# Four buffers for weight sums and split weights, splits three groups ahead, and another product order in the first MLP pair

## The chip, the core and the metric

The kernel runs on one core of a Trainium2 chip. A core has a matrix engine (TensorE, PE in the profile, with its weight loads shown apart as PEld), three engines for element work (VectorE or DVE, ScalarE or ACT, GpSimd or POOL), and SyncE (SP), which here issues nearly all DMA transfers. Each engine works through its own instructions in order and waits for the others on semaphores. Matmuls write to PSUM, everything else lives in SBUF. The metric is the device time of one execution in microseconds.

## The reference

One decoder layer over a sequence of 1024 positions with width 1024, in float32. Cut to what matters:

```python
h = rmsnorm(x, mix_norm)
proj = h @ w_in                                   # q, k, v, su, sv, g_a, g_b
y_att = sliding_window_attention(q, k, v, ...)     # 8 heads, window 128
y_sgu = chunked_spatial_gating(su, sv, ...)        # causal chunks of 128
merged = sigmoid(g_a) * (y_att @ w_oa) + sigmoid(g_b) * (y_sgu @ w_ob)
x = x + merged @ w_out
x = x + conv_gated_mlp(rmsnorm(x, ffn_norm), w_up, conv_w, conv_b, w_down)   # D_FF 2816
```

## The kernel before

**Arithmetic.** A float32 operand is split into a high part (a copy to the matmul's float type, on ACT, `copy_hi`, line 87) and a low part (operand less high part, on POOL or DVE), and a product is three matmuls: high by high, high by low, low by high. Besides, the large products are done in Strassen's manner as Winograd wrote it: a 2 by 2 block product with seven block products, named by the left operand (A11, A12, S1, S2, S3, S4, A22) with the right one (B11, B21, T1, T2, T3, B22, T4). In the gate and MLP stages a product (`prod`, line 1018) is 12 matmuls of 128 by 128 by 512. S1 to S4 are sums of weight blocks and must be made on the chip.

**Stages.** First come norm, projections, attention and spatial gating. Then eight gate pairs (one 128-row block of g_b and of g_a each; `gate_pair`, line 1112, makes the last seven, about 250 to 423 us), 16 jobs for the two branches (y @ w_ob and y @ w_oa, each times its gate, to 507 us), 14 groups for the output projection (`out_group`, line 1437, to 613 us), and 22 pairs of the MLP's up projection with its down projection between them. The first two MLP pairs are special: the first (`first_pair`, line 1570) finds its right operands only as the projection ends.

**Gate pairs and weight sums.** A gate pair computes A11, S3, A12, S1, A22, S2 and S4 in this order into halves of two PSUM tiles (zg with g0, g1 and zv with v0, v1). Its sums (`Blocks.sums`, 1029) and the scaling by the row norm run on DVE, its tanh on ACT (`gate_out`), from where the gate goes to DRAM. The next pair copies A11's result (x1, line 1124) to SBUF before A12 is added to the same PSUM half. In the same stage DVE prepares sums of weights that come later: 30 units, listed in `UNITS` (1044), a "u" unit for an MLP pair (two operations on 512 columns) and an "o" unit for the output projection (four on 256). A step (`sums_step`, 1066) first has SP load the next unit into one of two `ls` buffers (`sums_load`, 1051), then makes its own sums in place and stores them to DRAM (1077 for "u", 1084 for "o"). From the second of these pairs on there are three steps in a pair; the last ten units are made in the branches. In the sixth pair `ya_load` also fetches the attention's result (four loads).

**Jobs.** `run_jobs` (705) runs branches and output groups as one list. For job i it issues the matmuls, then the load of job i + 4, then, in an output group, the first part of the group's tail, then the split of job i + 2, and then the rest. An output group's tail is what its product releases (`ends` in `main`): `copies` after group 1 (M1 copied from one set of PSUM halves, X, to the other, Yb), `end_c11` after 3, `end_c22` after 9, `end_c12` after 11 and `end_c21` after 13. These add the residual, store x2, and build the MLP's right operands from it: high and low parts of B11, B21, B22 and T1 to T4. The last job of the list is `first_left`, which loads the first MLP pair's left operands; their splits (p for A11 and A12, s3, q for S1 and A22, and AX for S2 and S4) stand inside `end_c12`, `end_c21` and group 10's tail. A split weight (`woh`, `wol`) has two buffers.

**The first pair** makes A11, S3, S1, A12, S4, S2, A22. A11 and S2 share a PSUM half of zv with S3 and A22 beside it; copies to SBUF (x1, x7, u5, u2) free them.

The order of instructions within each engine is that of the program text; a tile framework puts the semaphores in.

## Time and profile before

| | us |
|---|---|
| median of 3 runs | 1277.44 (1274.58 to 1277.73) |
| the profiled execution | 1278.34 |
| its span | 1276.6 |
| PE busy in it | 1199.7 |
| DVE, POOL, ACT busy | 922.0, 588.3, 568.7 |
| mean granted PE clock | 0.974 |

The span runs from the first to the last instruction; 1.7 us lie around it. Where a row of a table by stage is cited, its start and end are us from the span's start. A row of the timeline gives start, length, engine, line, operation, out and in tiles with their shape, how many instructions it joins, and in brackets the idle time just before it with what ended it. SPq is SP's sequencer, where DMA issues stand in order.

### The profile page before, as it was taken

To read this page: it belongs to the slowest core of one execution; us is meant where nothing else is said; L and a number is where in the kernel's file an instruction comes from. 1 tells how busy PE (TensorE), PEld (TensorE's weight loads), DVE (VectorE), ACT (ScalarE), POOL (GpSimd) and SP (SyncE) were. 2 spreads that over 40 slices of the span, in tenths; PEclk is the share of its full clock that TensorE was granted. 3 is DMA by queue.
4 is the path that set the end of the run, shared out by engine and by line. 5 is a ranking of instruction groups with operands and counts; after the bars stand their busy time and mean duration, and the time that the engine had idled before them with its cause. 6 is when DMAs were issued, how large, how long until landed. Compare 5 with 4: busy or idle time off the path is not lost.

```text
span 1276.6 us, 16055 instructions
## 1 busy us (share of the span) xinstructions
PE 1199.7 (94%) x5842; PEld 1005.7 (79%) x5842; DVE 922.0 (72%) x1094; ACT 568.7 (45%) x883; POOL 588.3 (46%) x375
## 2 busy tenths in 40 slices
PE   8999999998897899995689999999999999999998
PEld 8989899876775688774467888888888888788887
DVE  7789948666547677474438887887887889686574
ACT  8555667623324112554344444444444445443432
POOL 2476673875556223353546566566566553000000
PEclk9999999999899899997789999999999999999999
DMA  7110150276786798642213233243233355986372
GB/s 269 31 38 32 53 217 16 69 244 226 236 294 208 267 338 300 205 168 74 74 42 116 99 125 126 106 132 122 99 119 129 109 178 185 368 300 206 117 227 94
DMA packets 92767, 202.82 MB, mean 159 GB/s; under 512 B 9744, under 2 KB 18192, under 8 KB 92688
## 3 DMA queue, kind: packets, MB, share of 16 engines
q1 hardware_dynamic: 92688, 201.80, 45.8%
q8 instruction: 46, 0.75, 0.2%
q14 instruction: 33, 0.27, 0.1%
HBM read 146.97 MB, written 54.79 MB: 158 GB/s over the span
## 4 chain that ended last, share of the span: by engine, by line
PE 63%; DVE 13%; DMA 6%; issue 6%; ACT 5%; POOL 4%; SPq 0%; ACTq 0%; POOLq 0%; DVEq 0%
PE pz L1022 32%; PE pd L1794 9%; PE pdy L1794 7%; DVE ls L620 3%; PE px L1450 3%; DMA ls<-wout 3%; DMA sum<-ls 2%; PE po L93 2%; PE po L91 2%; PE po L92 2%; POOL wol L1434 1%; DVE xa L620 1%; DVE pz L1038 1%; PE pu L93 1%; PE pu L91 1%
## 5 line engine op out<-in xcount | busy, mean ns | idle before, releaser
L1022 PE MATMUL pz<-T,qh 128*128 128x512 f32 x472 | 148.3, 396 | 5.4 <-DVE pz L1599 4.4
L620 DVE TENSOR_TENSOR ls<-ls 128x512 f32<-128x512 f32 (+1 forms) x76 | 81.4, 1071 | 58.5 <-DMA ls<-wup 29.8
L1022 PE MATMUL pz<-B,ph 128*128 128x512 f32 x352 | 110.0, 394 | 2.1 <-DVE tmp L1587 1.4
L982 POOL TENSOR_TENSOR pl<-lp,ph 128x1024 fp32r<-128x1024 f32 x30 | 72.2, 2407 | 86.1 <-ACT ph L87 85.9
L1022 PEld LDWEIGHTS pz<-T,qh 128*128 128x128 f32 x472 | 89.9, 191 | 25.4 <-DVE pz L1599 4.8
L1022 PE MATMUL pz<-T,ql 128*128 128x512 f32 x236 | 92.9, 394 | 0.0
L982 POOL TENSOR_TENSOR ql<-lq,qh 128x1024 fp32r<-128x1024 f32 x30 | 77.4, 2582 | 13.7 <-ACT qh L87 13.7
L1022 PE MATMUL pz<-T,s3h 128*128 128x512 f32 x232 | 73.4, 398 | 9.7 <-ACT tmp L1579 9.7
L1022 PEld LDWEIGHTS pz<-B,ph 128*128 128x128 f32 x352 | 65.4, 189 | 18.5 <-ACT x L1638 3.6
L1038 DVE TENSOR_TENSOR pz<-pz,rstd_b 128x1024 f32<-128x1024 f32 x60 | 74.0, 1232 | 7.4 <-ACT rstd_b L141 5.4
L982 POOL TENSOR_TENSOR s3l<-s,s3h 128x512 fp32r<-128x512 f32 x29 | 38.5, 1326 | 73.6 <-ACT s3h L87 73.6
L1022 PE MATMUL pz<-B,pl 128*128 128x512 f32 x176 | 68.6, 390 | 0.0
L1794 PE MATMUL pd<-bl,ah 128*128 128x512 f32 x176 | 68.5, 389 | 0.0
L1794 PE MATMUL pd<-bh,al 128*128 128x512 f32 x176 | 68.5, 389 | 0.0
L1794 PE MATMUL pd<-bh,ah 128*128 128x512 f32 x176 | 68.5, 389 | 0.0
L1022 PE MATMUL pz<-x,ph 128*128 128x512 f32 x128 | 45.6, 441 | 20.1 <-ACT x L1124 20.1
L1022 PE MATMUL pz<-B,AX 128*128 128x512 f32 x264 | 63.6, 390 | 0.8 <-DVE pz L1589 0.8
L1022 PE MATMUL pz<-T,AX 128*128 128x512 f32 x264 | 63.4, 389 | 0.0
L1434 POOL TENSOR_TENSOR wol<-wo,woh 128x1024 fp32r<-128x1024 f32 x14 | 34.5, 2465 | 55.9 <-ACT woh L87 55.9
L1022 PEld LDWEIGHTS pz<-T,s3h 128*128 128x128 f32 x232 | 44.5, 193 | 19.4 <-ACT tmp L1579 10.1
L1022 PEld LDWEIGHTS pz<-B,AX 128*128 128x128 f32 x264 | 49.5, 188 | 11.4 <-DVE pz L1589 1.2
L1022 PEld LDWEIGHTS pz<-T,AX 128*128 128x128 f32 x264 | 49.6, 188 | 10.3
(351 smaller groups left out, 3603.3 us busy)
## 6 DMA issues: line engine op xcount, KB each, us to landing
ls<-wup SPq DMA_DIRECT2D x22, 512.0 KB, 5.4
sum<-ls SPq DMA_DIRECT2D x22, 512.0 KB, 6.1
lp<-wup SPq DMA_DIRECT2D x22, 512.0 KB, 3.5
ra<-wdown SPq DMA_DIRECT2D x44, 256.0 KB, 5.0
b<-T SPq DMA_DIRECT2D x44, 256.0 KB, 4.0
B<-tv SPq DMA_DIRECT2D x33, 256.0 KB, 2.0
T<-tt SPq DMA_DIRECT2D x33, 256.0 KB, 2.0
b<-B SPq DMA_DIRECT2D x33, 256.0 KB, 3.3
```

Source lines behind the costliest of these rows:

```text
L91: nc.tensor.matmul(out, wh, mh, start=first, stop=False, **kw)
L92: nc.tensor.matmul(out, wh, ml, start=False, stop=False, **kw)
L93: nc.tensor.matmul(out, wl, mh, start=False, stop=last, **kw)
L620: eng.tensor_tensor(out, x, y, op=op)
L982: nc.gpsimd.tensor_tensor(l, r, h.bitcast(F), op=ALU.subtract)
L1022: nc.tensor.matmul(o, p[:, k, :], y[:, q, k, :], start=not more and k == 0 and j == 0, stop=k == 3 and j == 2, skip_group_check=True)
L1038: nc.vector.tensor_tensor(z, z, rstd_b, op=ALU.mult)
L1434: nc.gpsimd.tensor_tensor(l, r, h.bitcast(F), op=ALU.subtract)
L1450: nc.tensor.matmul(o[d], w[p][:, k, 128 * d:128 * d + 128], y[:, q, 2 * kp + k, :], start=s in ("M1", "M7") and kp == 0 and k == 0 and j == 0,
L1794: nc.tensor.matmul(o[d], p[:, k - k0, m], q[:, k - k0, :], start=new and k == 0 and j == 0, stop=k == HK - 1 and j == 2, skip_group_check= ...
```

## The change

The diff has three parts.

First, the weight sums. Units before the fourteenth rotate through four places, two `ls` buffers and two halves of a new tile `lsy` in the pool `big`; from unit 14 on the two `ls` buffers remain. `v_end` issues a second load, and step 12 issues none, so loads run two units ahead until then and one from there on. `ya_load` moves from the sixth pair to the seventh (c = 5 to c = 6), since the pool `big` has seven tiles.

On SP's queue, in the fourth of these gate pairs, before (`sum` is a unit's store to DRAM, `so` one of an "o" unit, `lq` the next pair's left operand, `dth` a gate's store):

```order
L1058 DMA ls_3558<-wup 128x512
L1059 DMA ls_3558<-wup 128x1024
L1077 DMA sum_3563<-ls_3511 128x1024
L97 DMA lq_3596<-wga 128x1024
L1097 DMA dth_3603<-th_3601 128x1024
L1062 DMA ls_3605<-wout 128x4x256
L1077 DMA sum_3609<-ls_3558 128x1024
L1058 DMA ls_3663<-wup 128x512
L1059 DMA ls_3663<-wup 128x1024
L1084 DMA so_2419<-ls_3605 512x1x256
```

The same stretch on SP's queue after the change:

```order
L1073 DMA ls_3558<-wout 128x4x256
L1089 DMA sum_3562<-lsy_3055 128x1024
L97 DMA lq_3595<-wga 128x1024
L1109 DMA dth_3602<-th_3600 128x1024
L1069 DMA lsy_3055<-wup 128x512
L1070 DMA lsy_3055<-wup 128x1024
L1089 DMA sum_3608<-ls_3511 128x1024
L1069 DMA lsy_3055<-wup 128x512
L1070 DMA lsy_3055<-wup 128x1024
L1096 DMA so_2419<-ls_3558 512x1x256
```

Each load now stands a step earlier: the "o" load that stood behind `lq` and `dth` stands ahead of both.

Second, the output projection. A group's preparation of others is put into a function `ahead`, which runs right after its matmuls and ahead of its whole tail: the right operand's split for group g + 2 (`m_prep`), the weight split for group g + 3, the load for group g + 6, the residual's load, and the first MLP pair's loads (group 10) and splits (groups 11 to 13). Split weights have four buffers: two `wst` ones, two halves of a tile `we`, and for groups 12 and 13 a tile `wl`. The squares' tile `sqt` moves to the pool `big`. The high and low parts of T2 move to the end of `end_c21`.

On ACT at groups 0 to 3, before (`woh` is a weight's high part, the copies of line 1330 are M1's, `rT` is m_prep's):

```order
L87 ACTIVATE woh_5000<-wo_4811 128x1024
L1330 COPY px_4966<-px_4964 128x512 x2
L1330 COPY px_4967<-px_4965 128x512
L87 ACTIVATE woh_5034<-wo_4851 128x1024
L1330 COPY px_4967<-px_4965 128x512
L87 ACTIVATE rT_645_5071<-m_4247 128x1024
L87 ACTIVATE woh_5074<-wo_4997 128x1024
```

And after:

```order
L87 ACTIVATE we<-wo_4806 128x1024
L87 ACTIVATE we<-wo_4846 128x1024
L87 ACTIVATE woh_5030<-wo_4997 128x1024
L1341 COPY px_4962<-px_4960 128x512 x2
L1341 COPY px_4963<-px_4961 128x512 x2
L87 ACTIVATE rT_638_5065<-m_4242 128x1024
L87 ACTIVATE woh_5068<-wo_5000 128x1024
```

Three weight splits (groups 2, 3 and 4) now stand ahead of M1's copies, and the four copies stand together. On ACT at group 11, ahead of C12's evacuation (its first copy is the last row), before:

```order
L87 ACTIVATE woh_5431<-wo_5321 128x1024
L87 ACTIVATE rT_679_5420<-m_4289 128x1024
L1386 COPY ac_5242<-px_4964 128x512
```

And after:

```order
L87 ACTIVATE rT_661_5400<-m_4284 128x1024
L87 ACTIVATE ph_5442<-lp_5405 128x1024
L87 ACTIVATE s3h_5446<-s_663_5407 128x512
L87 ACTIVATE qh_5450<-lq_5409 128x1024
L1388 COPY ac_5248<-px_4960 128x512
```

The first pair's three splits p, s3 and q have come ahead of this copy. On ACT at the end of C21 up to the copy of the first pair's A11 (x1, the last row in both), before:

```order
L1412 COPY ac_5066<-px_4967 128x512
L87 ACTIVATE B_692_5571<-px_4967,cp 128x512
L87 ACTIVATE T_693_5579<-px_4966 128x512
L87 ACTIVATE qh_5589<-lq_5417 128x1024
L87 ACTIVATE AX_5593<-lr_5495 128x1024
L1412 COPY ac_5066<-px_4967 128x512
L87 ACTIVATE B_692_5571<-px_4967,cp 128x512
L87 ACTIVATE T_693_5579<-px_4967 128x512 x2
L1579 COPY tmp<-pz_5613 128x512
```

And after:

```order
L1408 COPY ac_5075<-px_4963 128x512
L87 ACTIVATE B_675_5554<-px_4963,cp 128x512
L87 ACTIVATE T_676_5562<-px_4962 128x512
L1408 COPY ac_5075<-px_4963 128x512
L87 ACTIVATE B_675_5554<-px_4963,cp 128x512
L87 ACTIVATE T_676_5562<-px_4963 128x512 x2
L87 ACTIVATE T_677_5585<-traw_5454 128x512 x4
L1598 COPY tmp<-pz_5594 128x512
```

The two splits q and AX are gone from here, and four high parts of T2 have come.

Third, the first pair makes A11, S1, S3, A12, S2, S4, A22, so that its products alternate between the tiles zv and zg. The copy of S3's result (x7) is left out, and the squares of C12 stand ahead of S2's sum and those of C21 behind it, where all eight stood ahead of S4.

The diff:

```diff
@@ -705,13 +705,14 @@
     def run_jobs():
 
 
-        for i in range(len(jobs) - 1):
+        for i in range(len(jobs)):
             m = jobs[i][2](job_w.pop(i))
             next(m)
-            job_load(i + 4)
             if len(jobs[i]) > 3:
-                next(m)
-            job_split(i + 2)
+                jobs[i][3]()
+            else:
+                job_load(i + 4)
+                job_split(i + 2)
             for _ in m:
                 pass
 
@@ -865,6 +866,7 @@
         x_split("T4")
         nx.load_q()
         sums_load()
+        sums_load()
         q.prod(q.v1, "S2", "T2")
         nc.scalar.copy(x7, q.v0)
         nx.split_p()
@@ -1046,6 +1048,15 @@
     for c in range(6):
         UNITS += [("u", 2 * c), ("o", c + 2), ("u", 2 * c + 1)]
     UNITS += [("u", i) for i in range(12, NPAIR)]
+    ls_y = []
+
+    def ls_tile(n):
+        if not ls_y:
+            ls_y.append(Y("lsy", F, [128, 2, 2048]))
+        if n < 14 and n % 4 > 1:
+            return ls_y[0][:, n % 2, 0:1536]
+        return pools["ls"].tile([128, 1536], F, tag="ls", name=nm("ls"), bufs=2)
+
     d_so = [dr.tile([128, 4, 512], F, tag=f"so{k}", name=f"so{k}") for k in range(4)]
 
     def sums_load():
@@ -1054,11 +1065,11 @@
         if n < len(UNITS):
             kind, i = UNITS[n]
             if kind == "u":
-                x = pools["ls"].tile([128, 3, 4, 128], F, tag="ls", name=nm("ls"), bufs=2)
+                x = ls_tile(n).rearrange("p (a b c) -> p a b c", a=3, b=4)
                 nc.sync.dma_start(x[:, 0], a["wup"][2 * i][:, 0:4])
                 nc.sync.dma_start(x[:, 1:3], a["wup"][2 * i + 1].rearrange("p (b k) m -> p b k m", b=2))
             else:
-                x = pools["ls"].tile([128, 4, 256], F, tag="ls", name=nm("ls"), bufs=2)
+                x = ls_tile(n)[:, 0:1024].rearrange("p (a b) -> p a b", a=4)
                 nc.sync.dma_start(x, a["wout"][i // 2][:, :, 256 * (i % 2):256 * (i % 2) + 256])
             sums[n] = x
             sums["load"] += 1
@@ -1067,7 +1078,8 @@
 
         n = sums["make"]
         if n < len(UNITS):
-            sums_load()
+            if n != 12:
+                sums_load()
             kind, i = UNITS[n]
             x = sums.pop(n)
             if kind == "u":
@@ -1149,7 +1161,7 @@
         else:
             job_split(1)
             ya_split()
-        if c == 5:
+        if c == 6:
             ya_load()
         if c < 6:
             g_left[c + 2].load_p()
@@ -1264,7 +1276,7 @@
     HK = NPAIR // 2
     acs = {}
     X, Yb = [], []
-    traw = []
+    traw, ering, w_last = [], [], []
 
     def open_out():
         pools["ls_cm"].__exit__(None, None, None)
@@ -1273,6 +1285,7 @@
         pools["ex"] = ctx.enter_context(tc.tile_pool(name="ex", bufs=1, reuse_waits="tile"))
         pools["fp_cm"] = tc.tile_pool(name="fp", bufs=1, reuse_waits="tile")
         fp = pools["fp"] = pools["fp_cm"].__enter__()
+        ering.append(pools["ex"].tile([128, 2, 2, 2, 512], R, tag="T3", name="we"))
         pools["sq2"] = fp.tile([128, 1024], F, name="sq2")
         pools["ng2"] = fp.tile([128, 8], F, name="ng2")
         nc.vector.tensor_scalar(pools["ng2"], g2, -1.0, None, op0=ALU.mult)
@@ -1325,15 +1338,11 @@
 
     def copies():
         for d in range(4):
-            if d == 3:
-                yield
             nc.scalar.copy(Yb[d], X[d])
 
     def end_c11():
         t = acs["C11"]
         for d in range(4):
-            if d == 3:
-                yield
             half_add(Yb[d], Yb[d], t[:, d, :])
             nc.scalar.copy(t[:, d, :], Yb[d])
             x2_store("C11", d)
@@ -1347,11 +1356,9 @@
 
     def end_c22():
         t = acs["C22"]
-        sqt = pools["ex"].tile([128, 4, 512], F, tag="T3", name="sqt")
+        sqt = Y("sqt", F, [128, 2, 4, 512])[:, 0]
         sq2 = pools["sq2"][:, H]
         for d in range(4):
-            if d == 3:
-                yield
             half_add(t[:, d, :], X[d], t[:, d, :])
             x2_store("C22", d)
             hi("B22", d, t[:, d, :], gain(4 + d))
@@ -1375,13 +1382,8 @@
             lo("T1", d, X[d])
             nc.vector.tensor_tensor(tr[:, 1, d, :], h22[:, d, :], X[d], op=ALU.subtract)
             hi("T3", d, tr[:, 0, d, :])
-            hi("T2", d, tr[:, 1, d, :])
 
         for d in range(4):
-            if d == 3:
-                yield
-                lefts[0].sums_r()
-                lefts[0].split_p()
             half_add(X[d], X[d], t[:, d, :])
             nc.scalar.copy(t[:, d, :], X[d])
             x2_store("C12", d)
@@ -1402,12 +1404,6 @@
             hi("T4", d, Yb[d])
 
         for d in range(4):
-            if d == 3:
-                yield
-                lefts[0].split_q()
-                lefts[0].split_r(0)
-                for i in range(4):
-                    lo("T2", i, tr[:, 1, i, :], nc.gpsimd)
             half_add(Yb[d], Yb[d], t[:, d, :])
             nc.scalar.copy(t[:, d, :], Yb[d])
             x2_store("C21", d)
@@ -1419,6 +1415,9 @@
         late(3)
         lo("T4", 2, Yb[2])
         lo("T4", 3, Yb[3])
+        for d in range(4):
+            hi("T2", d, tr[:, 1, d, :])
+            lo("T2", d, tr[:, 1, d, :], nc.gpsimd)
 
     def out_load(g):
         s, _, b = OUT[g // 2]
@@ -1428,8 +1427,15 @@
             nc.sync.dma_start(t[:, j, :], (a["wout"][k] if s in ("M1", "M2", "M4") else d_so[k])[:, b, :])
         return t
 
-    def out_split(r):
-        h, l = (wst.tile([128, 2, 512], R, tag="w" + x, name=nm("wo" + x)) for x in "hl")
+    def out_split(g, r):
+        if g > 11:
+            if not w_last:
+                w_last.append(Y("wl", R, [128, 2, 2, 2, 512]))
+            h, l = (w_last[0][:, g % 2, x] for x in range(2))
+        elif g % 4 > 1:
+            h, l = (ering[0][:, g % 2, x] for x in range(2))
+        else:
+            h, l = (wst.tile([128, 2, 512], R, tag="w" + x, name=nm("wo" + x)) for x in "hl")
         copy_hi(h, r)
         nc.gpsimd.tensor_tensor(l, r, h.bitcast(F), op=ALU.subtract)
         return h, l
@@ -1451,20 +1457,13 @@
                                          start=s in ("M1", "M7") and kp == 0 and k == 0 and j == 0,
                                          stop=kp == 1 and k == 1 and j == 2, skip_group_check=True)
             yield
-            if g in (2, 4, 6):
-                ac_load({2: "C21", 4: "C22", 6: "C12"}[g])
-            if g + 2 < 14:
-                m_prep(g + 2)
             if g == 6:
                 scaled("C11", 0)
             if g == 10:
-                lefts[0].split_s3()
                 scaled("C22", 4)
             ends = {1: copies, 3: end_c11, 9: end_c22, 11: end_c12, 13: end_c21}
             if g in ends:
-                yield from ends[g]()
-            else:
-                yield
+                ends[g]()
             if g in (5, 7):
                 c, b = (("C21", X), ("C22", Yb))[g == 7]
                 for d in range(4):
@@ -1473,10 +1472,30 @@
                 for d in range(4):
                     lo("T3", d, traw[0][:, 0, d, :], nc.gpsimd)
 
-        jobs.append((lambda: out_load(g), out_split, main, True))
-
-    for g in range(14):
-        out_group(g)
+        def ahead():
+            w = lefts[0]
+            if g + 2 < 14:
+                m_prep(g + 2)
+            for i in (2, 3) if g == 0 else (g + 3,):
+                if i < 14:
+                    job_split(16 + i)
+            for i in (4, 5, 6) if g == 0 else (g + 6,):
+                if i < 14:
+                    job_load(16 + i)
+            if g in (2, 4, 6):
+                ac_load({2: "C21", 4: "C22", 6: "C12"}[g])
+            if g == 10:
+                first_left()
+            if g == 11:
+                w.split_p()
+                w.split_s3()
+                w.split_q()
+            if g == 12:
+                w.sums_r()
+            if g == 13:
+                w.split_r(0)
+
+        jobs.append((lambda: out_load(g), lambda r: out_split(g, r), main, ahead))
 
 
 
@@ -1578,25 +1597,24 @@
         q.prod(q.v1, "A11", "B11")
         nc.scalar.copy(x1, q.v1)
         nx.load_p()
-        q.prod(q.v0, "S3", "T3")
-        nc.scalar.copy(x7, q.v0)
+        q.prod(q.g1, "S1", "T1")
+        nc.scalar.copy(u5, q.g1)
         nx.load_q()
         nx.load_s3()
-        q.prod(q.g1, "S1", "T1")
-        nc.scalar.copy(u5, q.g1)
-        nc.vector.tensor_tensor(x7, x7, q.g1, op=ALU.add)
+        q.prod(q.v0, "S3", "T3")
+        nc.vector.tensor_tensor(x7, u5, q.v0, op=ALU.add)
         q.prod(q.g0, "A12", "B21")
         nc.vector.tensor_tensor(q.g0, x1, q.g0, op=ALU.add)
         nx.split_p()
         nx.split_s3()
         for d in range(4):
-            sq_add("C21", d, Yb[d])
-        for d in range(4):
             sq_add("C12", d, Yb[d])
-        q.prod(q.g1, "S4", "B22", more=True)
         q.prod(q.v1, "S2", "T2", more=True)
         nc.scalar.copy(u2, q.v1)
         nc.vector.tensor_tensor(q.v1, x7, q.v1, op=ALU.add)
+        for d in range(4):
+            sq_add("C21", d, Yb[d])
+        q.prod(q.g1, "S4", "B22", more=True)
         nx.sums_r()
         nx.split_q()
         lefts[2].load_p()
@@ -1891,7 +1909,8 @@
             if g == 0:
                 q.tanh()
 
-    jobs.append((first_left, lambda w: w, None))
+    for g in range(14):
+        out_group(g)
     with tc.manual_schedule():
         v_phase()
         psum["H"] = None
```

## The prediction

> **What bounds the kernel now.** I read the page's span and engine table first.
>
> ```profile
> span 1276.6 us, 16055 instructions
> PE 1199.7 (94%) x5842; PEld 1005.7 (79%) x5842; DVE 922.0 (72%) x1094; ACT 568.7 (45%) x883; POOL 588.3 (46%) x375
> ```
>
> PE is busy for 94% of the span, so whatever is to be gained lies in PE's waits and in matmuls run at a slow clock. The second view is the list of waits, PE's longest (us in total, times, longest).
>
> ```profile
> PE pz L1022 <- ACT x L1124: 20.1, 6, 4.8
> PE px L1450 <- ACT woh L87: 10.5, 3, 6.6
> PE pz L1022 <- ACT tmp L1579: 9.7, 1, 9.7
> PE px L1450 <- POOL wol L1434: 6.7, 5, 1.9
> PE pz L1022 <- DVE pz L1599: 4.4, 1, 4.4
> ```
>
> The first row lies in the gate pairs, the second and fourth in the output projection, the third and fifth in the first MLP pair: the three places that the diff touches. The third view is the table by stage. I cut the gate pairs where PE resumes after each wait, which is the A12 product of each pair; the columns are length, then each engine's busy time, PE's granted clock, DMA share and GB/s.
>
> ```profile
> 273.40:294.30 20.90, 19.39 (x85) 15.71 (x85) 13.60 (x15) 7.20 (x10) 14.56 (x8) 1.00 0.64 214
> 294.30:317.96 23.66, 19.33 (x84) 15.68 (x84) 13.11 (x16) 7.18 (x10) 14.06 (x8) 0.98 0.74 244
> 317.96:343.95 25.99, 22.05 (x84) 17.66 (x85) 15.16 (x16) 7.30 (x10) 13.89 (x8) 0.89 0.66 222
> 343.95:368.08 24.13, 20.96 (x84) 16.83 (x84) 14.24 (x16) 7.29 (x10) 14.09 (x8) 0.93 0.77 257
> 368.08:395.21 27.13, 21.25 (x84) 16.79 (x84) 13.82 (x16) 7.29 (x10) 13.98 (x8) 0.94 0.71 256
> 395.21:428.42 33.21, 26.66 (x108) 21.26 (x108) 26.09 (x21) 14.46 (x18) 17.83 (x7) 0.92 0.61 203
> 428.42:507.20 78.78, 78.64 (x337) 64.49 (x338) 55.30 (x58) 13.35 (x22) 22.05 (x15) 0.97 0.93 335
> 507.20:612.80 105.60, 88.03 (x338) 68.90 (x337) 63.02 (x68) 54.48 (x78) 46.89 (x23) 0.89 0.43 145
> 612.80:685.00 72.20, 54.19 (x225) 42.91 (x223) 36.37 (x46) 28.52 (x41) 35.60 (x21) 0.88 0.22 72
> 685.00:704.00 19.00, 19.00 (x84) 15.66 (x84) 16.95 (x17) 8.33 (x10) 12.19 (x6) 1.00 0.36 120
> ```
>
> The last row is the floor: 84 matmuls in 19.00 us, 0.226 each, at a clock of 1.00. Against it the five gate windows before 395.21 lose 121.81 − 95.0 = 26.8 us, the output projection (336 matmuls, 76.0 us) loses 29.6, and the first two MLP pairs also run far above it. The branches between (428.42 to 507.20) have no room.
>
> **Weight sums in the gate pairs.** The views are the waits of SP's queue, the timeline, and landing times of loads.
>
> ```profile
> SPq L1058 <- DMA sum<-ls: 57.5, 14, 6.4
> ls<-wout SPq DMA_DIRECT2D x5, 512.0 KB, 5.9
> 273.40 0.74 PE L1022 MATMUL pz<-x,ph 128*128 128x512 f32 x2 [2.34 <-ACT x L1124]
> 282.02 6.67 DVE L620 TENSOR_TENSOR ls<-ls 128x256 f32<-128x256 f32 x4 [2.06 <-DMA ls<-wout]
> 294.29 0.73 PE L1022 MATMUL pz<-x,ph 128*128 128x512 f32 x2 [1.51 <-ACT x L1124]
> 301.47 0.60 SPq L1062 DMA_DIRECT2D ls<-wout  x1
> 307.48 4.89 DVE L620 TENSOR_TENSOR ls<-ls 128x256 f32<-128x256 f32 x4 [5.19 <-DMA ls<-wout]
> 317.96 1.22 PE L1022 MATMUL pz<-x,ph 128*128 128x512 f32 x2 [4.34 <-ACT x L1124]
> 395.21 1.00 PE L1022 MATMUL pz<-x,ph 128*128 128x512 f32 x2 [4.83 <-ACT x L1124]
> 409.92 9.63 DVE L620 TENSOR_TENSOR ls<-ls 128x256 f32<-128x256 f32 x4
> ```
>
> With two buffers a load waits on SP until the store out of its buffer has landed (14 times, 57.5 us) and then takes 5.9. In the second of these windows SP issues it at 301.47 and DVE stands 5.19 us until 307.48. Behind that step on DVE lie the pair's sums and scale, behind these on ACT the tanh of zv and then the next pair's x1 copy, for which A12 waits. The lag is steady: the step ends at 288.69 and PE resumes at 294.29, it ends at 312.37 and PE resumes at 317.96, 5.6 us both times. So no gap needs the step to end by 19.05 − 5.6 = 13.4 us after A12.
>
> The change issues loads two units ahead into four buffers, so the load for this step is there. It can then start once S1 is done and x7 is added, 2 × 2.72 + 0.7 = 6.1 us after A12. With 4.89 to 6.67 us it ends at 11.0 to 12.8, in time by 0.6 to 2.4 us; at the 9.63 of the seventh pair it would end at 15.8, 2.4 late. PE sets the pace at 4.9 to 6.7. The four windows from 273.40 to 368.08 (94.68 us) become 4 × 19.0 = 76.2 plus what small waits and clock remain; I take 80.5, gain 14.2. The gap of 2.34 ahead of 273.40 goes too: it has the same cause. The next window (27.13) keeps part: its unit 15 is again in the two-buffer rule, whose wait there is the 4.83, and the four loads of ya now stand in this pair; with the step's load issued earlier than now I take 24 (gain 3). The seventh pair I leave at nothing: its DVE, 26.09 us busy in 33.21, is the cover and stays. Sum 19.5; ends 5 (below) and 26.8 + 2.3 = 29.
>
> **The ring of split weights.** Views: timeline and landing times at the end of the projection.
>
> ```profile
> wo<-so SPq DMA_DIRECT2D x8, 256.0 KB, 4.0
> 589.33 0.58 ACT L1386 COPY ac<-px 128x512 f32<-128x512 f32 x1 [3.21 <-DVE px L1299]
> 601.19 1.04 ACT L87 ACTIVATE woh<-wo 128x1024 fp32r<-128x1024 f32 x1
> 602.13 1.04 ACT L87 ACTIVATE ph<-lp 128x1024 fp32r<-128x1024 f32 x1
> 602.28 1.22 PE L1450 MATMUL px<-rT,woh 128*128 128x512 f32 x2 [6.60 <-ACT woh L87]
> 607.08 1.83 ACT L87 ACTIVATE T<-traw 128x512 fp32r<-128x512 f32 x3 [0.83 <-DVE traw L1376]
> 607.56 0.68 DVE L1376 TENSOR_TENSOR traw<-ac,px 128x512 f32<-128x512 f32 x1
> 609.44 0.70 DVE L1299 SCALAR_TENSOR_TENSOR px<-px,ac 128x512 f32<-128x512 f32 x1 [1.20 <-PE px L1450]
> 624.53 0.58 ACT L1579 COPY tmp<-pz 128x512 f32<-128x512 f32 x1
> 625.17 1.22 PE L1022 MATMUL pz<-T,s3h 128*128 128x512 f32 x2 [9.69 <-ACT tmp L1579]
> ```
>
> Now group 13's split (601.19) stands on ACT behind three quarters of C12's evacuation, and PE waits 6.60 us for it. With splits three groups ahead, these waits go. A new one comes: group 4's split, whose load starts only in group 0, now stands ahead of M1's copies on ACT, for which group 2 waits; between 0 and the 4.0 of a landing, I take 2. PE then ends group 13 at 507.2 + 76.0 + 2 = 585 instead of 612.8, 28 us earlier.
>
> That is not the gain, since ACT and DVE are late next. C12's first copy now stands on ACT behind the end of C22 and behind rT, group 13's split, rT, ph, qh (5 × 1.04), four scaled copies (4 × 0.58) and s3h (0.6), 8.1 us. Group 9 ends at 507.2 + 54.3 + 2 = 563.5, its last square some 2 us later, so the copy starts at 573.6 (589.33 before). C12's own chain runs on DVE from there to 608.24, 18.9 us; the last copy no longer stands behind woh and ph (1.85 from 601.19 to the end less the overlap), so 17.05: 590.7. C21's chain now takes 15.1 us from 609.44 to the x1 copy at 624.53. The change puts four T2 splits (0.61 each from the T row, 2.45) ahead of that copy and takes qh and the AX split away, of which I count 0.4: 17.15, and with 0.25 to start, x1 is copied at 608.1 and S3 starts at 608.7. Gain there 625.17 − 608.7 = 16.4. PE has done A11 and S1 by 593 and stands some 15 us.
>
> **The first pair's order.** The chain of waits gives PE's runs of matmuls.
>
> ```profile
> 625.17 8.48 PE pz L1022 x24
> 648.96 1.22 PE L1022 MATMUL pz<-T,qh 128*128 128x512 f32 x2 [4.37 <-DVE pz L1599]
> 657.47 1.68 PE pz L1485 x16
> ```
>
> From S3 to the next pair's sums of squares 32.3 us pass, in which PE makes seven products of 12 matmuls (S3, S1, A12, S4, S2, A22 and the next pair's A11). After the change S1 is done before S3, and six are left: S3 and A12 take 8.5 (the 24 matmuls of the first row, slow after a wait: 3.05 over the floor's 5.43), to 617.2; S2 and S4 2 × 2.72, to 622.7; S2's sum on DVE, with only four of the eight squares ahead of it, reaches 624.4; A22 and the next A11 take 6.4, an estimate between the floor's 5.43 and the 8.5 from 648.96 on, since the wait ahead of them shrinks from 4.37 to 1.7: 630.8. That is 22 us, gain 10 more. One ACT copy (x7, 0.58) drops, beside other work: nothing. The moved squares cost nothing while S4 covers them; uncovered, 4 × 0.7. So projection and first pair gain 26; ends 12 (rival C) and 30.
>
> [...] The row: after 4.34 idle the 84 matmuls from 317.96 took 22.05, 3.05 over 19.00, and after 9.69 idle 24 took 3.05 over; the loss doesn't grow with the wait, so I charge S3's longer wait once. [...]
>
> **Sum.** 19.5 + 26 = 45.5 off the profiled execution's 1278.34 is 1232.8. The median of the runs, 1277.44, lies 0.9 lower; I say 1233.
>
> **Rivals.** B: DVE's weight-sum step grows once loads, POOL's splits and stores lie closer together, as in the seventh pair (9.63 for the same four operations). Against it: 4.89 and 6.67 at full DMA traffic in the earlier pairs. At 9.63 each pair ends 2.4 late with a clock loss of up to 1.5, near 22.5 us; four pairs 90, gain 5, total 31: 1247. [...]
>
> C: first_left's four loads land late and its three splits hold C12's copies on ACT, or A22 still finds its sum late: of the 26 some 12 stay, 1247. The loads have 573.6 − 8.1 = 565.5 to about 571; the 4.0 landing speaks against it.
>
> A second way to lose: the gates gain nothing since the transfer is hidden behind another limit (B with lq as the late load), and only the projection gains: 1252. I count it with B.
>
> D, slower: ACT is in order and a group's split now stands ahead of its ends. A load has three groups (16.3 us) against 4.0 now; if it landed later than that, every copy and each PE group would wait. To eat 45 us over the 11 groups it must be 4.1 late each, a landing of over 20 us. The DMA share of 0.43 there against 0.93 in the branches speaks against it.
>
> **Chances.** The forecast 0.62, B 0.18, C 0.10, B and C together (1261) 0.03, D past break-even (over 1281) 0.05, within 0.3% (3.8 us, about what a measurement tells from no change) 0.02. The bounds of the forecast alone are 1220 (gates 26, projection 30) and 1243. Down to 1220 and up to 1254, which takes in B and C, leaves out under 2 in 10. Faster 0.93, same 0.02, slower 0.05.
>
> **What would show it.** Right: the wait on the x1 copy in the gates is under 5 us, windows of 84 matmuls near 19 to 20 at a clock near 1; no wait on woh or wol; a single wait on the first pair's copy, of 13 to 18 us, ahead of S3; no wait on its DVE sum above 2. Wrong: weight-sum steps of over 8 us or loads of ls that land late; C12's first copy later than 577 + the gates' shift; SP's queue standing on stores in the projection.

## The result

The changed kernel takes 1236.31 us (median of 4 runs, 1235.52 to 1238.62) against 1276.16 before (median of 4 runs; the 1277.44 given ahead of the prediction is that of three of them): a ratio of 0.9691 with a 95% interval of 0.9671 to 0.9711, 39.85 us less. The profiled execution's span went from 1276.6 to 1234.8 us.

The page's first lines and PE's waits, in the order of the prediction's:

```profile
span 1234.8 us, 16059 instructions
PE 1180.9 (96%) x5842; PEld 995.3 (81%) x5842; DVE 932.0 (75%) x1094; ACT 568.0 (46%) x882; POOL 592.9 (48%) x375
```

```profile
PE pz L1024 <- ACT tmp L1598: 12.7, 1, 12.7
PE pz L1024 <- ACT x L1136: 4.8, 1, 4.8
PE pz L1024 <- DVE x L1154: 4.5, 1, 4.5
PE pz L1024 <- DVE traw L1383: 4.4, 2, 2.8
PE px L1456 <- DVE ac L1312: 3.4, 1, 3.4
```

The waits on woh and wol are gone from the list. Of the six waits on x1 in the gates one is left, and the one ahead of S3 has grown from 9.7 to 12.7. Two rows are new among the longest: PE waits 3.4 us in the projection for DVE's additions to C22 (`ac`; 0.4 before), and 4.4 in two for the sums of which T1 is made (`traw`). The latter lie ahead of S3's long wait and cost nothing while that stands. The table by stage, cut at A12 of each gate pair, then at the start of the branches, of the projection, at S3 and at the end of the first pair:

```profile
271.12:290.16 19.04, 19.04 (x86) 15.77 (x84) 15.02 (x13) 6.74 (x9) 13.91 (x9) 1.00 0.74 264
290.16:309.20 19.04, 19.04 (x86) 15.77 (x84) 15.89 (x15) 7.21 (x9) 14.38 (x9) 1.00 0.79 293
309.20:329.01 19.81, 19.33 (x85) 15.69 (x84) 15.15 (x18) 7.42 (x9) 13.01 (x8) 1.00 0.82 263
329.01:348.74 19.73, 19.37 (x85) 15.69 (x84) 13.24 (x15) 7.22 (x9) 13.85 (x9) 1.00 0.67 250
348.74:373.45 24.71, 19.50 (x85) 15.50 (x84) 13.59 (x16) 6.47 (x10) 15.82 (x9) 0.99 0.82 265
487.58:595.30 107.72, 84.62 (x361) 68.05 (x359) 78.39 (x82) 61.58 (x90) 58.85 (x28) 0.93 0.48 161
595.30:614.88 19.58, 18.20 (x73) 14.60 (x73) 8.00 (x12) 7.95 (x13) 10.37 (x8) 0.92 0.09 28
```

Four gate pairs now run within 0.8 us of the floor, with the clock at 1.00. The projection's first matmul stands at 487.58 (507.16 before, 19.6 earlier). From there to S3 it takes 107.72 us (118.01 before, 10.3 less), and from S3 to the next pair's sums of squares 19.58 (32.14 before, to PE's first matmul of them at 657.31; 12.6 less). Those three add up to 42.4 before rounding; 0.6 of it is given back in the MLP.

Where the projection's end goes is seen in the timeline of ACT, DVE and PE around C22 and C12, and at S3:

```profile
540.68 6.73 DVE L1247 TENSOR_TENSOR rB<-m,rB 128x1024 fp32r<-128x1024 f32 x2
547.34 2.47 DVE L1312 SCALAR_TENSOR_TENSOR ac<-px,ac 128x512 f32<-128x512 f32 x4
548.05 0.72 ACT L87 ACTIVATE B<-ac,cp 128x512 fp32r<-128x512 f32 x1 [6.19 <-DVE ac L1312]
548.76 11.15 PE L1456 MATMUL px<-rB,we 128*128 128x512 f32 x48 [3.42 <-DVE ac L1312]
552.08 0.62 ACT L1365 ACTIVATE sqt<-ac 128x512 f32<-128x512 f32 x1
560.76 0.59 ACT L1388 COPY ac<-px 128x512 f32<-128x512 f32 x1 [0.35 <-DVE px L1312]
592.60 2.18 ACT L87 ACTIVATE T<-traw 128x512 fp32r<-128x512 f32 x4
594.68 0.57 ACT L1598 COPY tmp<-pz 128x512 f32<-128x512 f32 x1
595.30 1.22 PE L1024 MATMUL pz<-T,s3h 128*128 128x512 f32 x2 [12.70 <-ACT tmp L1598]
```

C22's four additions on DVE stand behind two low parts of right operands (m_prep for groups 10 and 11), of 3.4 us each. ACT has idled 6.19 us when the first addition is done, and PE 3.42; C22's high parts and squares then take ACT to 552.7, and C12's first copy follows at 560.76.

### The profile page after: what moved, and what is told of

Read it like the earlier page. It is cut to its first block, busy times and chain, and to the rows that moved or that the text cites. A ratio compares the mean times of both kernels' runs of the same rounds, so it can differ in the third digit from the quotient of the medians.

```text
span 1234.8 us, 16059 instructions
## 1 busy us (share of the span) xinstructions
PE 1180.9 (96%) x5842; PEld 995.3 (81%) x5842; DVE 932.0 (75%) x1094; ACT 568.0 (46%) x882; POOL 592.9 (48%) x375
## 4 chain that ended last, share of the span: by engine, by line
PE 48%; DVE 2%; ACT 1%; issue 1%; ACTq 0%; DVEq 0%
PE pz L1024 31%; PE pd L1812 9%; PE pdy L1812 7%; DVE sq L1337 0%; DVE res L1832 0%; DVE tg L1525 0%; DVE pz L1040 0%; ACT tv L1520 0%; DVE tt L620 0%; PE pz L138 0%; ACT px L1336 0%; PE pz L1504 0%; DVE tv L1525 0%; DVE pz L1548 0%; DVE tv L1549 0%
## 5 line engine op out<-in xcount | busy, mean ns | idle before, releaser
L1024 PE MATMUL pz<-T,s3h 128*128 128x512 f32 x232 | 72.6, 395 | 12.7 <-ACT tmp L1598 12.7
L1024 PEld LDWEIGHTS pz<-B,ph 128*128 128x128 f32 x352 | 65.1, 188 | 18.4 <-ACT x L1656 3.5
L620 DVE TENSOR_TENSOR ls<-ls 128x512 f32<-128x512 f32 (+1 forms) x60 | 58.5, 975 | 25.5 <-DMA ls<-wup 16.0
L1024 PEld LDWEIGHTS pz<-B,AX 128*128 128x128 f32 x264 | 49.6, 188 | 10.3
L1024 PEld LDWEIGHTS pz<-T,AX 128*128 128x128 f32 x264 | 49.5, 188 | 10.3
L1525 DVE SCALAR_TENSOR_TENSOR tv<-pz,cp,tv 128x1023 f32<-128x1023 f32 (+1 forms) x44 | 56.2, 1278 | 0.8
L1525 DVE SCALAR_TENSOR_TENSOR tg<-pz,cp,tg 128x1023 f32<-128x1023 f32 (+1 forms) x44 | 56.2, 1278 | 0.8
```

What stands on the lines that cost most here:

```text
L620: eng.tensor_tensor(out, x, y, op=op)
L1024: nc.tensor.matmul(o, p[:, k, :], y[:, q, k, :], start=not more and k == 0 and j == 0, stop=k == 3 and j == 2, skip_group_check=True)
L1525: nc.vector.scalar_tensor_tensor(t[:, j:], p[:, 0:1024 - j], cw[:, ci, 2 - j:3 - j], t[:, j:], op0=ALU.mult, op1=ALU.add)
```

## The experiments

All ratios are to the kernel before in runs on the same chip, with their 95% intervals.

### The two halves alone

`sums_only` is the kernel before with the first part of the diff:

```diff
+    def ls_tile(n):
...
         nx.load_q()
         sums_load()
+        sums_load()
...
-        if c == 5:
+        if c == 6:
             ya_load()
```

> The kernel before with the first part of the change alone (four buffers for weight sums, loads two units ahead, ya one pair later). Theory: the gates' gain is its own, 19.6 us from the first matmul on to the output projection as in the changed kernel, so the projection's first matmul at about 487.6 instead of 507.16, the waits on woh and wol unchanged near 17 us, and a time of 1276.2 - 19.6 = 1256.6 (1254 to 1259). Rival: the two halves need each other (the earlier projection runs into loads that are late, or part of the gates' gain is given back in the branches): 1261 or more.

Measured: 1257.44 us, ratio 0.9844 (0.9821 to 0.9867); the projection's first matmul stands at 487.66 and the waits on woh and wol are 10.4 and 6.7. `proj_only` is the changed kernel with `sums_load`, `sums_step` and `ya_load` of before:

> The changed kernel with the weight sums of before (two buffers, one unit ahead, ya in the sixth pair). Theory: projection and first pair keep their 22 us, since they begin with a stage that the gates don't reach into: 1276.2 - 22 = 1254 (1252 to 1257), with gate waits on the x1 copy near 20 us again. Rival: part of these 22 us comes from sums that were stored earlier (the loads of so): then 1258 or more.

Measured: 1255.83 us, ratio 0.9837 (0.9814 to 0.9859). The two parts save 19.1 and 20.7 us, which add up to the whole change's 39.85 well within the intervals: no run shows that one needs the other.

### Four buffers without the lead

`one_ahead` keeps the four buffers and takes back the lead:

```diff
         nx.load_q()
         sums_load()
-        sums_load()
...
-            if n != 12:
-                sums_load()
+            sums_load()
```

> The changed kernel with its four buffers, but loads one unit ahead instead of two. Theory: what cost time was the load's wait for the store out of its own buffer, not the lead; with the wait gone a load one step ahead has some 8 us against a landing of 5.9, so at least 15 of the gates' 19.6 us stay: 1236 to 1241. Rival: the lead of two units is what matters, since SP reaches a load only behind the stores and gate stores ahead of it: gaps of 2 to 4 us in each pair come back, 1246 or more.

Measured: 1255.64 us, ratio 0.9837 (0.9810 to 0.9863), the same as with two buffers (`proj_only`). My theory fell: the buffers alone are worth nothing that these runs can tell. Three rows of SP and DVE in this kernel say why:

```profile
296.43 0.55 SPq L1107 DMA_DIRECT2D dth<-th  x1
297.03 0.90 SPq L1072 DMA_DIRECT2D lsy<-wout  x1
305.07 6.95 DVE L620 TENSOR_TENSOR lsy<-lsy 128x256 f32<-128x256 f32 x4 [3.16 <-DMA lsy<-wout]
```

No store out of the load's own buffer is waited for any more in these pairs. But the load stands on SP right behind the second gate store of the pair (`dth`), which waits for ACT's tanh (SP stood 26.7 us in nine such waits); DVE then waits 3.16 us for it, and PE's waits on x1 are 16.9 us in five. In the changed kernel, with the lead, the load for the step of that pair stands behind the first gate store instead and 8 us earlier:

```profile
288.53 0.33 SPq L1109 DMA_DIRECT2D dth<-th  x1
288.95 0.60 SPq L1073 DMA_DIRECT2D lsy<-wout  x1
296.47 5.83 DVE L620 TENSOR_TENSOR lsy<-lsy 128x256 f32<-128x256 f32 x4
```

### Gate stores off SP's queue

The new theory was that the gate's store holds the load. Two kernels move it in `gate_out` to ACT's queue, one with four buffers and one unit ahead, one with two buffers and the rest as in `proj_only`:

```diff
-        nc.sync.dma_start(d, t)
+        nc.scalar.dma_start(d, t)
```

> Four buffers, one unit ahead (1255.6 us), and the gates' stores issued from ACT's queue, right behind the tanh that makes them, instead of SP's. Theory, formed after that run: a load one unit ahead stands on SP behind the gate's store, which waits for ACT's tanh; there the load of an o unit left at 297.03 right behind the store at 296.43. With the store gone from SP the load leaves some 3 to 5 us earlier, and most of the lost 19 us come back: 1238 to 1243. Rival: loads are late because of the landing time itself and of SP's other waits (stores of sums, lq), so the lead of two units is needed anyway: 1250 or more.

> Two buffers and one unit ahead as before, projection and first pair as in the changed kernel (1255.8 us), and the gates' stores issued from ACT's queue. Theory: with two buffers the load still waits for the store out of its own buffer (53.5 us of SP's time), so little is won: 1251 to 1257, and the wait of SP's loads on stores of sums grows. Rival: the gate's store alone was what held the loads, and buffers do nothing: 1238 to 1243, as with four.

Measured: 1248.53 us, ratio 0.9791 (0.9775 to 0.9807), with four, and 1248.16, ratio 0.9781 (0.9761 to 0.9801), with two. Both expectations missed. The gate store's place is worth 0.5 to 0.6% in either case (6 to 7 us of the 19), so it is one cause; but with it gone the loads are still late, and two buffers do as well as four. What is left is a load that leaves a step ahead at most. With four buffers, in this stretch of `one_ahead_actq`:

```profile
335.01 0.33 SPq L1087 DMA_DIRECT2D sum<-lsy  x1
335.44 0.41 SPq L97 DMA_DIRECT2D lq<-wga  x1
335.89 1.23 SPq L1072 DMA_DIRECT2D ls<-wout  x1
345.50 6.55 DVE L620 TENSOR_TENSOR ls<-ls 128x256 f32<-128x256 f32 x4 [3.21 <-DMA ls<-wout]
```

The load now leaves right behind lq, and comes 9.6 us later, 3.21 too late, although nothing of its own stands before it. Its landing in these pairs takes 7.2 us on the median (5.9 before), and that of lq beside it 6.8. What holds its start is the store ahead of lq: it is the store of the previous unit's sums, which DVE ended at 334.99. With a lead of one a load stands on SP behind that store, so here it could not leave before the step two before its own was done. So in this order of SP's queue the 19 us belong to the lead of two units, and more than two buffers are what makes that lead possible (three were not run). How the remaining 13 us split between landing time and queue was not tried further; the stores of sums on another engine's queue would be the test.

### The order of the first pair

`old_order` has the products and squares of before in `first_pair`:

```diff
         q.prod(q.v1, "A11", "B11")
...
+        q.prod(q.v0, "S3", "T3")
+        nc.scalar.copy(x7, q.v0)
...
         q.prod(q.g1, "S1", "T1")
         nc.scalar.copy(u5, q.g1)
+        nc.vector.tensor_tensor(x7, x7, q.g1, op=ALU.add)
-        q.prod(q.v0, "S3", "T3")
-        nc.vector.tensor_tensor(x7, u5, q.v0, op=ALU.add)
...
+        for d in range(4):
+            sq_add("C21", d, Yb[d])
         for d in range(4):
             sq_add("C12", d, Yb[d])
+        q.prod(q.g1, "S4", "B22", more=True)
         q.prod(q.v1, "S2", "T2", more=True)
```

> The changed kernel with the first MLP pair's products and squares in the order of before. Theory: S3 starts where it starts now (about 595.3), since it waits for the x1 copy in either order; then S1 stands behind it instead of ahead (2.7 us), the sum behind S1 and A12 opens small waits (2 us) and S2's sum again stands behind eight squares (a wait of some 4 us ahead of A22): 8 to 11 us slower than the changed kernel, 1244 to 1247. Rival: only the one product counts, 2.7 us, and the squares' place is hidden: 1239.

Measured: 1247.99 us, ratio 0.9770 (0.9748 to 0.9793), 11.7 us above the changed kernel, a little more than the theory's range. Its PE timeline has S3 at the same place, a wait behind each step, and the end 11.3 us later (626.21 against 614.88):

```profile
595.27 1.22 PE L1024 MATMUL pz<-T,s3h 128*128 128x512 f32 x2 [19.96 <-ACT tmp L1598]
604.36 0.73 PE L1024 MATMUL pz<-B,ph 128*128 128x512 f32 x2 [1.40 <-DVE tmp L1606]
608.17 3.01 PE L1024 MATMUL pz<-B,AX 128*128 128x512 f32 x12 [0.79 <-DVE pz L1608]
618.30 1.22 PE L1024 MATMUL pz<-T,qh 128*128 128x512 f32 x2 [4.40 <-DVE pz L1618]
```

The new order's share of what projection and first pair gain is thus about half; the second part of the diff brings the rest. Which of its pieces does so, the four buffers for split weights, the lead of three groups or the place of `ahead` in front of the tail, was not tested apart.

### What S3 waits for

`t2_early` puts T2's splits back into `end_c12`:

```diff
             hi("T3", d, tr[:, 0, d, :])
+            hi("T2", d, tr[:, 1, d, :])
+            lo("T2", d, tr[:, 1, d, :], nc.gpsimd)
...
         lo("T4", 3, Yb[3])
-        for d in range(4):
-            hi("T2", d, tr[:, 1, d, :])
-            lo("T2", d, tr[:, 1, d, :], nc.gpsimd)
```

> The changed kernel with the high and low parts of T2 made inside C12's evacuation again. Theory: the four T2 splits at the end of C21 (592.60, 2.18 us) stand on the path to the x1 copy for which S3 waits, while C12's chain is paced by DVE and takes them for nothing: S3 2.2 us earlier, 1234 (1233 to 1235). Rival: they hold C12's chain on ACT by as much, 1236.

Measured: 1238.64 us, ratio 0.9716 (0.9700 to 0.9733), no faster. POOL is why: T2's low parts now stand ahead of the sums for S2 and S4 (`lr`), ACT's split of these waits for them, and C21's copies stand behind it:

```profile
581.00 1.06 ACT L87 ACTIVATE AX<-lr 128x1024 fp32r<-128x1024 f32 x1 [4.01 <-POOL lr L620]
```

In the changed kernel this split started at 576.43 without a wait, though its projection began 3.1 us later. The 2.18 us saved ahead of x1 were more than lost there: counted from C12's first copy, C21's first copy came 5.0 us later than in the changed kernel and S3 2.9. `x1_early` leaves T2 and moves A11, S1 and their copies from `first_pair` into the third turn of `end_c21`'s loop:

```diff
+    def first_begin():
...
+        q.prod(q.v1, "A11", "B11")
+        nc.scalar.copy(x1, q.v1)
+        q.prod(q.g1, "S1", "T1")
+        nc.scalar.copy(u5, q.g1)
...
         for d in range(4):
+            if d == 2:
+                first_begin()
             half_add(Yb[d], Yb[d], t[:, d, :])
```

> The changed kernel with the copies x1 and u5 (results of A11 and S1, on PE done by 582) put into the middle of C21's evacuation on ACT instead of behind it. Theory: S3 has its operand long before and waits only for x1, which stands in ACT's queue; S3 then runs near 584, A12 follows when B21's last low part is there (591.4), and the 12.7 us wait falls to some 8 in two pieces: about 6 us off, 1230 (1228 to 1232). Rival: T2's splits, still behind C21, become what S2 waits for and keep half: 1233.

Measured: 1229.52 us, ratio 0.9639 (0.9625 to 0.9654). S3 now runs at 583.70 and the long wait is gone:

```profile
583.70 0.73 PE L1024 MATMUL pz<-T,s3h 128*128 128x512 f32 x2 [0.83 <-ACT tmp L1602]
589.08 0.50 PE L1024 MATMUL pz<-B,ph 128*128 128x512 f32 x1 [0.77 <-DVE B L1318]
591.16 0.50 PE L1024 MATMUL pz<-B,ph 128*128 128x512 f32 x1 [1.12 <-DVE B L1318]
594.46 5.46 PE L1024 MATMUL pz<-T,AX 128*128 128x512 f32 x12 [2.57 <-DVE tmp L1614]
```

The wait of 12.7 us was for a copy of 0.57 us that stood late in a queue: its source, A11's result, lies in PSUM from 575.3 on in the changed kernel and from 574.6 in `x1_early`. (S3 writes the other half of the tile that this copy reads; why it waits for that copy at all, no run shows.) Counted from the projection's start S3 comes 10.5 us earlier and the end of the first pair 5.5: the rest goes into the waits behind S3.

### C22's place on DVE

`c22_first` moves one low part behind C22's additions:

```diff
-            if g + 2 < 14:
+            if g == 9:
+                m_hi(11)
+            elif g + 2 < 14:
                 m_prep(g + 2)
...
                 nc.gpsimd.tensor_tensor(sq2, sq2, sqt[:, d, :], op=ALU.add)
+        m_lo(11)
         for d in range(4):
             lo_gain("B22", d, t[:, d, :], gain(4 + d))
```

> The changed kernel with the low part of group 11's right operand (one of the two rB operations on DVE at 540.68, 6.73 us for both) behind C22's four additions instead of ahead of them; its high part stays. Theory: C22's evacuation is late because it stands on DVE behind two such operations, each at 3.4 us beside POOL's weight splits; with one out of the way the additions start at 544 instead of 547.34, PE's wait of 3.42 ahead of group 10 falls under 0.5, C12's first copy (560.76) comes 3 us earlier, and the time is 3 us less: 1233 (1232 to 1234 beside 1236). Rival: the ACT queue ahead of C12 (8.1 us) or group 11's product sets the copy, and nothing is won: 1236.

Measured: 1235.48 us, ratio 0.9681 (0.9653 to 0.9708), which can't be told from the changed kernel's 0.9691. The wait of 3.42 us is gone from PE's list, as expected, but C12's first copy came only 0.7 us earlier from the projection's start (558.58 − 486.13 against 560.76 − 487.58). A new wait took the place:

```profile
546.50 8.01 DVE L1328 SCALAR_TENSOR_TENSOR B<-ac,cp,B 128x512 fp32r<-128x512 f32 x4
554.58 0.72 ACT L1385 ACTIVATE ac<-ac,cp 128x512 f32<-128x512 f32 x1 [2.08 <-DVE B L1328]
```

The scaling of C22 overwrites what B22's low parts still read, and these four operations took 8.01 us beside POOL's work. `no_low_split` asks what POOL does to DVE:

```diff
         copy_hi(h, r)
-        nc.gpsimd.tensor_tensor(l, r, h.bitcast(F), op=ALU.subtract)
+        if g not in (10, 11):
+            nc.gpsimd.tensor_tensor(l, r, h.bitcast(F), op=ALU.subtract)
```

> The changed kernel without POOL's low parts of the weights of groups 10 and 11 (the two operations from 538.14, 4.88 us): those groups multiply by the low parts that lie in the buffers from groups 6 and 7, so this part of the computation is left out. Nothing else changes on DVE. Theory: DVE's two rB operations in that stretch take 3.4 us each because POOL works beside them; without POOL's they take 1.2 to 1.3 as on their own, C22's additions start where group 9's product lets them (about 543 to 545 instead of 547.34), and PE's wait of 3.42 ahead of group 10 falls under 1.5. Rival: 3.4 us is what these operations take in this place (their operands, or DMA traffic), and nothing moves.

Measured: 1233.53 us, ratio 0.9676 (0.9657 to 0.9695). In the timeline:

```profile
538.99 2.35 DVE L1247 TENSOR_TENSOR rB<-m,rB 128x1024 fp32r<-128x1024 f32 x2
541.25 1.28 DVE L1312 SCALAR_TENSOR_TENSOR ac<-px,ac 128x512 f32<-128x512 f32 x2
543.71 1.29 DVE L1312 SCALAR_TENSOR_TENSOR ac<-px,ac 128x512 f32<-128x512 f32 x2 [1.17 <-PE px L1457]
544.92 7.59 DVE L1318 SCALAR_TENSOR_TENSOR B<-ac,cp,B 128x512 fp32r<-128x512 f32 x4
```

The theory holds: the two operations take 2.35 us instead of 6.73, DVE then waits for PE and not PE for DVE, and C12's first copy comes 2.5 us earlier from the projection's start (70.64 against 73.18). The time alone can't be told from the changed kernel's 0.9691. Next in line, the B22 parts again run beside POOL (7.59 us). A DVE operation on 128 by 1024 took 1.21 us with POOL idle (at 529.11 in the changed kernel) and 3.43 beside POOL's, and in these rows the one of the two that began later took the longer. Two rows of the changed kernel and one of `no_low_split`:

```profile
532.44 2.50 POOL L1440 TENSOR_TENSOR wol<-wo,woh 128x1024 fp32r<-128x1024 f32 x1 [3.37 <-ACT woh L87]
532.59 3.43 DVE L620 TENSOR_TENSOR m<-m,m 128x1024 f32<-128x1024 f32 x1
540.24 3.37 POOL L1441 TENSOR_TENSOR wl<-wo,wl 128x1024 fp32r<-128x1024 f32 x1 [7.00 <-ACT wl L87]
```

In the first two POOL began 0.15 us ahead and took 2.50 (2.41 at 559.00 in `no_low_split`); DVE ended at 536.02, 1.1 us after POOL. In the third, DVE's second low part (540.1, 1.22 us) was under way, and POOL took 3.37.

### The last gap, and everything together

`units16` keeps four buffers and the lead for two more units:

```diff
-        if n < 14 and n % 4 > 1:
+        if n < 16 and n % 4 > 1:
...
-            if n != 12:
+            if n != 14:
                 sums_load()
```

> The changed kernel with four buffers and two units of lead kept for two more units (14 and 15 in the second pair of buffers). Theory: the one gap that is left in the gates (4.83 us ahead of 373.45) is unit 15's, the first with a lead of one; with the lead it goes, with some clock loss after it, and the next pair gives at most 2 back: 1231 to 1233. Rival: ya's four loads, which need the place of these buffers, then come later, and the seventh pair lengthens by as much: 1236.

Measured: 1231.81 us, ratio 0.9644 (0.9622 to 0.9667), 4.5 us under the changed kernel. The gap of 4.83 is gone, and the seventh pair waits 5.84 us for x7 on DVE instead of 4.46, so little of it is given back. `best` joins what the runs pointed to. To the edits of `c22_first`, `units16` and `x1_early` it adds these, in `end_c22`, `end_c21` (where `first_mid` makes S3 and x7's sum) and `first_pair`:

```diff
-            hi("B22", d, t[:, d, :], gain(4 + d))
-            lo_gain("B22", d, t[:, d, :], gain(4 + d))
...
             hi("B21", d, Yb[d], gain(4 + d))
+            hi("T2", d, tr[:, 1, d, :])
+            lo("T2", d, tr[:, 1, d, :], nc.gpsimd)
...
+        first_mid()
         late(3)
...
         nx.load_p()
+        for d in range(4):
+            hi("B22", d, acs["C22"][:, d, :])
+            lo("B22", d, acs["C22"][:, d, :])
```

> Everything that the runs point to, on the changed kernel: the two edits of c22_first and units16, x1 and u5 copied in the middle of C21 (x1_early), x7's sum ahead of C21's last parts, one T2 split behind each of C21's four B21 splits (ACT waits 1.2 to 1.5 us for DVE there), and B22's high and low parts behind C21, from the scaled C22, where only S4 needs them. Theory: 3 for the gates' last gap, 5 for C12's copy, 6 for x1, 4 for S2, which in x1_early waited 2.57 us for x7 and ran 5.46 us instead of 2.72 beside T2's low parts: 18 us, 1218 (1214 to 1223). Rival: group 11's product then holds C12's first copy and B22's splits hold S4, and half of it stays: 1227.

Measured: 1220.03 us, ratio 0.9555 (0.9536 to 0.9574): 16 us under the changed kernel and 55.6 under the one before, inside the expected range, though the share of each of its edits was not measured. S3 waits 3.35 us, and no wait in projection and first pair is longer:

```profile
567.63 0.70 PE L1024 MATMUL pz<-T,qh 128*128 128x512 f32 x2 [2.83 <-DVE traw L1391]
574.00 1.22 PE L1024 MATMUL pz<-T,s3h 128*128 128x512 f32 x2 [3.35 <-ACT tmp L1612]
588.19 2.98 PE L1024 MATMUL pz<-B,AX 128*128 128x512 f32 x12 [2.26 <-DVE pz L1632]
592.80 0.73 PE L1024 MATMUL pz<-T,qh 128*128 128x512 f32 x2 [1.63 <-DVE pz L1639]
```

With B22's parts out of its way, C12's first copy (550.36, the projection starting at 482.10) comes at 68.3 instead of 73.2; `c22_first` alone had brought 0.7 of that.

## Why the prediction was right, and where it was not

The time forecast was 1233 and came out at 1236.31, inside the range, with the forecast case and not a rival. The sum was rounded up on its way (16.4 and 10 are 26.4, not 26, and the 0.9 by which the median lies lower was not taken off): its own terms give 1231.5. That the total came within 5 us is in part luck, since the projection fell 6.1 us short and the first pair gave 2.6 more. By its steps:

**Gates, 19.5 forecast, 19.6 measured.** The size is right partly by errors that cancel. The four windows came to 77.62 us instead of 80.5, so they gained 17.1, not 14.2; the first gap gave its 2.3; the sixth pair took 24.71 against 24 forecast, with the 4.83 of unit 15 in it; and the stretch from there to the projection, left at nothing, lost 2.2 (114.13 against 111.95). The ground was only partly right. I named the store out of the load's own buffer as what delays the load. `one_ahead` shows that removing that wait alone gains nothing, since the load then stands behind the gate's store, and the pair with ACT's queue shows that this is not all of it either: the lead of two units is what pays. I had quoted the rows on the store's wait, and not asked what stood next in SP's queue.

**Projection to S3, 16.4 forecast, 10.3 measured.** The failing step is "Group 9 ends at 507.2 + 54.3 + 2 = 563.5, its last square some 2 us later". From the projection's start group 9 ended at 57.8 instead of 56.3 (the wait for M1's copies, put at 2, took 2.2). C22's additions waited another 2.0 for the two operations of m_prep on DVE, and C22's high parts and squares then took ACT 5.4 from the first addition to the last square, where I had put 2 for all. Together the last square came at 65.1 instead of 58.3, 6.8 late. Rows of the kernel before had the size already:

```profile
566.00 2.47 DVE L1299 SCALAR_TENSOR_TENSOR ac<-px,ac 128x512 f32<-128x512 f32 x4
571.69 0.61 ACT L1358 ACTIVATE sqt<-ac 128x512 f32<-128x512 f32 x1
```

From the first addition to the end of the last square that is 6.3 us, with one weight split of 1.04 among them. The rest of that chain was as sized: 8.1 us of ACT work up to C12's first copy (8.06 measured), 17.05 for C12 (17.2), 17.4 with its start for C21 to the x1 copy (16.75). The two m_prep operations were on the path because of what `no_low_split` showed, POOL beside them, which I had weighed only for the gates (rival B), where it didn't decide.

**First pair, 10 forecast, 12.6 measured.** S3 and A12 took 7.0 us, not 8.5, and A22 and A11 5.6, not 6.4. `old_order` confirms the mechanism, with S3 at the same place.

**The signs.** Those of being right came, but for the wait ahead of S3, 12.7 instead of 13 to 18. Of those of being wrong, loads of `ls` landed more than 0.6 us late only where the lead is one (DVE waited 5.71 and 4.43 us for them in the sixth pair), and SP's queue stood on stores of x2 for 20.0 us in the projection's end, as it had before for 14.0, with no weight split late behind them. The one that counts came: C12's first copy was to come no later than 577 less the gates' 19.6, 557.4, and came at 560.76. It points at the step above.

**The clock.** I charged 3.05 for resuming after S3's wait because two rows of before showed it (the 24 matmuls from 625.17 at a granted clock of 0.66, the 84 from 317.96 at 0.87). Here 24 matmuls after 12.70 us took 7.00 to the start of the next, at 0.78, a loss of 1.56; in `old_order`, after 19.96, they took 7.69 (to 602.96, the end of the last), a loss of 2.25. These four losses lie between 1.56 and 3.05 and don't follow the wait's length, and my single value was their upper end.

**Rivals.** B did not come (DVE's step took 6.00 and 5.83 us in the first and second of the windows); for its clock loss of up to 1.5 a pair I had named no row, and the granted clock in the four windows was 1.00. C came in part, by another cause: not first_left's loads (C12's first copy waited 0.35, for DVE), but what stood ahead of them. D did not come: no wait on a weight split is left.

## What to carry to other kernels

A wait that a profile names can be only the last of several: before counting its removal as a gain, ask what stands next in the same queue, and test the buffer and the lead apart, since here the buffers without the lead gave nothing (1255.64 us against 1255.83). With the splits moved earlier, the evacuation chains behind them became the bound here (PE's wait ahead of S3 went from 9.7 to 12.7 us), so size these by each instruction that stands on the in-order engine, DVE's beside POOL's at the price measured there (3.4 us instead of 1.2). And a short copy behind a long chain in an in-order queue held the matrix engine for over twenty times its length here (0.57 us, 12.70): put it where its source is ready.

## What the runs showed of the hardware

An addition or subtraction of 128 by 1024 on DVE took 1.21 us with POOL idle (529.11 in the changed kernel) and 3.43 when POOL worked on a like operation that had begun first (532.59), and where DVE's began first, POOL's took 3.37 (540.24 in `no_low_split`) instead of 2.41 (559.00 there); with two of POOL's taken out, two of DVE's took 2.35 us in all instead of 6.73. I had weighed this for the gates and it mattered in the projection. After waits of 9.69, 12.70 and 19.96 us the next 24 matmuls took 3.05, 1.56 and 2.25 us longer than at the floor. After waits of the same length the same 48 matmuls took different times: after 3.42 us in the changed kernel their row is 11.15 us long (granted clock 1.00 from 548.76 to 559.74), after 3.42 us in `old_order` 12.51, and after 3.40 us in `units16` 11.13.
